# Split-array score products and split-array attention in a two-layer encoder trunk

## The chip, the cores and the metric

The kernel runs on one core of one Trainium2 chip. The metric is the device time of one execution in microseconds (us). A core has five engines with queues of their own: TensorE (matrix products; the profile lists its multiplications as PE and its loads of weights as PEld), VectorE (DVE), ScalarE (ACT), GpSimd (POOL) and SyncE (SP, which only issues DMAs here). Matrix products read SBUF and write PSUM, of which there are eight banks; the kernel hands them out one at a time (`ps`).

## The reference

A trunk of two layers is applied to two sequences of 512 and 256 tokens, 1024 wide, in float32. Each layer is half a gated feed-forward block, a token mixer, and half a feed-forward block again, each with a norm ahead of it and added to the residual:

```python
x = x + 0.5 * swiglu_ffn(rmsnorm(x, norm_g[li, 0]), ffn_w1[li, 0], ffn_w2[li, 0])
x = x + mixer(rmsnorm(x, norm_g[li, 1]))
x = x + 0.5 * swiglu_ffn(rmsnorm(x, norm_g[li, 2]), ffn_w1[li, 1], ffn_w2[li, 1])
```

The mixer of the first layer is a gated linear recurrence, run forwards and backwards with 8 heads of 128 by 128:

```python
# S_t = diag(f_t) S_{t-1} + k_t v_t^T,  o_t = S_t^T q_t,  f_t = lb + (1 - lb) sigmoid(.),  k_t = 1 - f_t
o = scan(q, k_f, i, logf_f) + reversed(scan(reversed(q), reversed(k_b), reversed(i), reversed(logf_b)))
o = (o * rsqrt(mean(o * o) + eps) * g_norm) * silu(g)
return o @ w_o
```

The mixer of the second layer is attention over a window of 128 tokens on both sides, with 16 query heads of 64, 4 key and value heads, rotation of the first 16 of each head's 64 dimensions, and one sink logit per head that joins the maximum and the denominator:

```python
s = einsum(q, k_band) * 64 ** -0.5, masked to |kpos - qpos| <= 128
m = max(max(s), sink)
p = exp(s - m);  denom = sum(p) + exp(sink - m)
o = (p / denom) @ v_band
return o @ w_o
```

## The kernel before

**Precision.** Most products are made of float32r operands: a float32 number is written as a high part `hi` (ScalarE copies and rounds, `split`, L263) and a remainder `lo` (VectorE subtracts, L264), and `mm3` (L256 to L260) adds hi x hi, hi x lo and lo x hi in PSUM. A float32r product is one record of TensorE in the profile; a product of float32 operands is two.

**Order of the work.** `tile_trunk_kernel` writes the stages one after the other: feed-forward, recurrence (`hgrn`), two feed-forward blocks, attention (`swa`), feed-forward. Inside a stage the order is written out by hand; the framework places the instructions on each engine's queue by that order and by what is ready, and adds the waits. The weights stream in through four raw buffers and are split ahead of their use.

**The recurrence.** `hgrn` (L803) makes the values, then for each head the query, and the two gates (`hgrn_proj`), then the scan (`hgrn_scan`, L676). The scan is woven with the projections of the next head (`weave`, L611): after each level of the scan, TensorE gets some pieces of those projections. The 768 tokens stand as six blocks of 128. The scan builds the matrix A of scores of each block by levels: at level l, of 0 to 6, groups of J = 2^l tokens attend to the neighbouring group, one direction for the left half and the other for the right. At each level

- ScalarE copies the keys of this level into `kop` (L699), a buffer that each level writes again;
- `scan_scores` (L670) makes one 128 x 128 product of float32 for each of the six blocks (L674): weights are the block of `kop`, data are the queries, read in place by a pattern of runs of J elements that alternates between the two directions' planes (`rhs`, L701); results go to two PSUM banks, four blocks in one and two in the other;
- `put` (L684) moves them to A, at level 0 by a copy (L688), else by a copy under a mask (L693), one instruction per bank;
- VectorE multiplies the queries (L716) and the keys (L720) in place by the gates' products, and makes the next level's products (L722).

Level 0 has a second set of scores, the diagonal, from `qs` and `kd`. After the levels come states (L744 to L755) and outputs (L768).

**Attention.** `swa` (L915) projects the keys and values; `put_kv` (L922) rotates each block of keys, splits it, writes high and low part twice each, and turns it by eight float32r transposes (`transpose_r`, L912, record line L913) into `kT`, which has the high part on both halves of the partitions and the low part likewise. Values are kept as high | low, 128 wide (`vv`). Then 24 units (4 groups of heads x 6 blocks of queries) go through `pipeline` (L1048), which sorts events by a step and a rank written out by hand, together with pieces of the query projections and, later, of the output projection. A unit (`Unit`, L1075) does

- `query`: split the four heads' queries into high | low (L263, L264); `turn`: four float32r transposes, and a copy out by ScalarE (L1100);
- `scores`, per head: two products over 128 rows (high and low query against the high part, and against the low part, of the keys; L1109, L1110), 256 or 384 keys wide; VectorE adds the band and takes the minimum (L1112);
- `exps` (L1125), `sink`, `denominator` (L1141);
- `probs`, per block of 128 keys: four float32 transposes (L1147), and a split of the result (L263, L264);
- `values`, per block: two products of 512 columns (L1159, L1160), high | low values against the high and the low probabilities;
- `finish`: ScalarE copies the lower half of the partitions (L1165) and VectorE adds it to the upper one (L1170).

`split_out` (L977) splits a group's outputs for the output projection (L986, L987), which `out_proj` (L1006) makes.

Of the kernel before, what the change touches and what calls it, by code (L numbers as in the profile page):

```python
# [47 lines left out]
class Trunk:  # L48
# [621 lines left out]
    def scan_scores(self, pss, lhs, rhs):  # L670
        nc = self.nc
        for b in range(NBLK):
            s, i = (0, b) if b < 4 else (1, b - 4)
            nc.tensor.matmul(pss[s][:, i * P : (i + 1) * P], lhs(b), rhs(b), start=True, stop=True)  # L674

    def hgrn_scan(self, hd, v):  # L676
# [7 lines left out]
        def put(level, pss):  # L684
            for s, (off, n) in enumerate(SEQS):
                dst = A[:, off : off + n]
                if level == 0:
                    nc.vector.tensor_copy(dst, pss[s])  # L688
                    continue
                nb = n // P  # L690
                m = self.masks[:, level, :].unsqueeze(1).to_broadcast([P, nb, P])
                r = lambda t: t.rearrange("p (b j) -> p b j", b=nb)
                nc.vector.copy_predicated(r(dst), m, r(pss[s]))  # L693

        tot, base = f, 0
        for l in range(LEVELS):
            c, J = T >> l, 1 << l
            kv = bass.AP(k.tensor, k.offset, [list(k.ap[0]), [2 * J, c // 2], [T + J, 2], [1, J]])
            nc.scalar.copy(kop.rearrange("p (b g j) -> p b g j", g=2, j=J), kv)  # L699

            def rhs(b):  # L701
                return bass.AP(
                    q.tensor, q.offset + b * P, [list(q.ap[0]), [2 * J, P // (2 * J)], [T + J, 2], [1, J]]
                )

            pss = [self.ps(n) for _, n in SEQS]
            self.scan_scores(pss, lambda b: blk(kop, b), rhs)
            put(l, pss)
            if l == 0:
                pss = [self.ps(n) for _, n in SEQS]  # L710
                self.scan_scores(pss, lambda b: blk(kd, b), lambda b: blk(qs, b))
                put(LEVELS, pss)
# [90 lines left out]
    def hgrn(self, lb_row, gn_row, next_row):  # L803
# [92 lines left out]
        self.drain(self.out_proj("hg_o", 0, uT, None))  # L896
        self.drain(self.out_proj("hg_o", 1, uT, next_row))

    def rotate(self, ps, heads, pos, t):
        nc = self.nc  # L900
        v = lambda t: t.rearrange("p (h d) -> p h d", d=HD)
        x, tv = v(ps), v(t)
# [12 lines left out]
    def swa(self, next_row):  # L915
# [3 lines left out]
        kT = [self.big([P, 2, T], F32R) for _ in range(KV)]  # L919
        vv = [self.big([P, 3, KV, P], F32R) for _ in range(2)]  # L920

        def put_kv(s, b, ps):  # L922
            off, n = SEQS[s]
            gb = off // P + b
            st = self.big([P, KV, 2, P], F32R)
            kh, kl = st[:, :, 0, :], st[:, :, 1, :]
            k = self.tmp(256)
            self.rotate(ps[:, :256], KV, b, k)
            self.split(k.rearrange("p (h d) -> p h d", d=HD), kh[:, :, :HD], kl[:, :, :HD])
            nc.scalar.copy(kh[:, :, HD:], kh[:, :, :HD].bitcast(F32))  # L930
            nc.scalar.copy(kl[:, :, HD:], kl[:, :, :HD].bitcast(F32))
            src = ps[:, 256:].rearrange("p (g d) -> p g d", d=HD)
            v = vv[gb // 3][:, gb % 3]
            nc.scalar.copy(v[:, :, :HD], src)
            nc.vector.tensor_sub(v[:, :, HD:], src, v[:, :, :HD].bitcast(F32))

            def rest():
                for g in range(KV):
                    pt = self.ps(256)
                    for i in range(2):  # L940
                        self.transpose_r(pt[:, i * P : (i + 1) * P], st[:, g, i, :])
                    nc.scalar.copy(kT[g][:, :, gb * P : (gb + 1) * P], pt.rearrange("p (a b) -> p a b", a=2))

            return rest
# [4 lines left out]
        def put_q(half):  # L949
            def f(s, b, ps):  # L950
# [4 lines left out]
                self.rotate(ps, 512 // HD, b, t)  # L955
# [6 lines left out]
        tiles = [None] * NC  # L962
        of = {}

        def units(gs):
            def alloc(g):
                if g not in of:
                    of[g] = self.big([P, 2, T])
                return of[g]
# [7 lines left out]
        def split_out(gs):  # L977
            for g in gs:
                for i in range(2):
                    for s, (off, n) in enumerate(SEQS):  # L980
                        if s == 0:
                            tiles[2 * g + i] = self.big([P, 2, T], F32R)
                        t = tiles[2 * g + i]
                        hi, lo = t[:, 0, off : off + n], t[:, 1, off : off + n]
                        src = of[g][:, i, off : off + n]
                        nc.scalar.copy(hi, src)  # L986
                        nc.vector.tensor_sub(lo, src, hi.bitcast(F32))  # L987

        q = itertools.chain(self.proj_tok("q0", put_q(0)), self.proj_tok("q1", put_q(1)))
        wo = self.out_proj("sw_o", 0, tiles, None)  # L990
# [6 lines left out]
        extra.append((60, lambda: split_out((0,))))  # L997
        extra.append((65, lambda: split_out((1,))))
        extra += [(66 + i * 5 / 4, piece(wo)) for i in range(24)]
        extra.append((84, lambda: split_out((2,))))  # L1000
        self.pipeline(list(units(range(KV))), extra)
        split_out((3,))
        self.drain(wo)
        self.drain(self.out_proj("sw_o", 1, tiles, next_row))

    def out_proj(self, tag, half, act, next_row):  # L1006
        for c in range(2):
            for b in range(NBLK):
                ps = self.ps()
                sl = slice(b * P, (b + 1) * P)  # L1010
                for i in range(4):
                    key = (tag, half, c, i // 2)
                    wh, wl = self.take(key)
                    t = act[half * 4 + i]
# [33 lines left out]
    def pipeline(self, units, extra):  # L1048
# [5 lines left out]
        for i, u in enumerate(units):  # L1054
# [3 lines left out]
            for h in range(GQ):  # L1058
                at(t + h // 2, 0, lambda u=u, h=h: u.scores(h))
# [15 lines left out]
class Unit:  # L1075
# [76 lines left out]
    def values(self, j):  # L1152
        k, nc = self.k, self.k.nc
        if j == 0:
            self.po = k.ps()
# [129 lines left out]
```

## Time and profile before

| | us |
|---|---|
| median of 3 runs (2833.03 to 3576.69) | 2833.57 |
| the profiled execution | 2833.56 |
| its span, first to last instruction | 2831.8 |
| recurrence, scan of the eight heads | 582 to 960 |
| attention, the units' pipeline | 2115 to 2304 |

The profile is of one execution. Its busy line gives the time that each engine worked and its share of the span; its chain follows the last instruction back through what released it. A group of instructions is named by line, engine, operation, what it writes <- what it reads, and shapes; behind the first bar stand the time that the group took in all and the mean of one in ns, behind the second bar the idle time of its engine ahead of it, and what ended that. In the view by stretches each engine has its busy time and its instruction count. In the timeline and the chain's pieces the first number is the start and the second the time taken; matrix products overlap in the pipeline, so the distance from start to start is the rate, and the time taken is longer.

### The profile page before, as it was taken

The page shows a single profiled execution, that of the slowest core. Times are in us where ns is not written, and L with a number is a line of the kernel's source. Part 1 is how long each engine was busy: PE and PEld are TensorE (multiplying, and loading weights), DVE is VectorE, ACT ScalarE, POOL GpSimd, SP SyncE. Part 2 cuts the span into 40 slices and gives each one's busy share as a digit, 9 for nine tenths or more (in the row PEclk, how much of TensorE's full clock was granted, in tenths as well). Part 3 has the DMA queues.
Part 4 walks back from the last instruction along what each step waited for, and adds up shares of the span by engine and source line. Part 5 has one row for each costly group of instructions (what it writes and reads, how often), then busy time and mean ns, then how long its engine had stood idle before and what let it go on. Part 6 is the DMA issues. An engine that isn't in the chain of part 4 may idle for free.

```text
span 2831.8 us, 40534 instructions
## 1 busy us (share of the span) xinstructions
PE 2790.5 (99%) x15225; PEld 2559.2 (90%) x15225; DVE 2203.1 (78%) x3846; ACT 1320.2 (47%) x2453; POOL 307.3 (11%) x306
## 2 busy tenths in 40 slices
PE   8999999999999999999999999999999899999998
PEld 8999999889899889999999999999887779999998
DVE  7888788477577558888878887887859978878877
ACT  7444443434344336444444643444457756434443
POOL 1111111000000001111111111111100001111110
PEclk9999999999999999999999999999999999999999
DMA  5554554311111133555454355554412113555543
GB/s 157 133 126 119 124 140 122 112 45 38 43 40 38 60 97 75 140 131 122 120 121 119 82 142 129 123 122 112 144 60 75 40 43 82 142 132 121 122 113 108
DMA packets 330100, 291.37 MB, mean 103 GB/s; under 512 B 11608, under 2 KB 257840, under 8 KB 329904
## 3 DMA queue, kind: packets, MB, share of 16 engines
q1 hardware_dynamic: 294064, 212.43, 25.6%
q0 software_dynamic: 31680, 62.93, 13.3%
q10 hardware_dynamic: 4160, 13.42, 1.3%
q8 instruction: 119, 1.95, 0.3%
q14 instruction: 77, 0.63, 0.1%
HBM read 216.39 MB, written 9.44 MB: 80 GB/s over the span
## 4 chain that ended last, share of the span: by engine, by line
PE 91%; DVE 6%; ACT 2%; issue 1%; DMA 0%; DVEq 0%; ACTq 0%; SPq 0%
PE ps L418 38%; PE ps L482 20%; PE ps L259 8%; PE ps L258 8%; PE ps L260 8%; PE ps L674 3%; PE ps L768 1%; DVE w L200 1%; DVE big L264 1%; PE ps L320 1%; PE ps L1147 1%; PE ps L744 1%; DVE w L167 0%; PE ps L1109 0%; DVE big L1112 0%
## 5 line engine op out<-in xcount | busy, mean ns | idle before, releaser
L418 PE MATMUL ps<-big,w 128*128 128x384 f32 x6720 | 1173.8, 335 | 1.5 <-ACT tA L435 1.4
L418 PEld LDWEIGHTS ps<-big,w 128*128 128x128 f32 x6720 | 1165.2, 188 | 8.4 <-ACT tA L435 6.4
L199 ACT CAST w<-wr 128x512 fp32r<-128x512 f32 x600 | 416.1, 707 | 689.2 <-DVE wr L213 342.8
L200 DVE TENSOR_TENSOR w<-wr,w 128x512 fp32r<-128x512 f32 (+1 forms) x520 | 447.8, 865 | 185.8 <-ACT w L199 174.8
L482 PE MATMUL ps<-w,big 128*128 128x512 f32 x2520 | 576.6, 390 | 0.7 <-DVE x L504 0.6
L482 PEld LDWEIGHTS ps<-w,big 128*128 128x128 f32 x2520 | 472.1, 188 | 100.1 <-ACT big L263 1.5
L504 DVE SCALAR_TENSOR_TENSOR x<-ps,x 128x512 f32<-128x512 f32 x468 | 304.3, 683 | 10.8 <-PE ps L260 10.0
L141 POOL DMA_DIRECT2D s<-wr x120 | 105.3, 877 | 1821.2 <-DMA wr<-in_ffn_w_dram 649.6
L258 PE MATMUL ps<-w,big 128*128 128x512 f32 x624 | 248.9, 399 | 0.3
L260 PE MATMUL ps<-w,big 128*128 128x512 f32 x624 | 244.9, 393 | 1.8 <-DVE big L327 1.0
L259 PE MATMUL ps<-w,big 128*128 128x512 f32 x624 | 244.2, 391 | 0.0
L258 PE MATMUL ps<-big,w 128*128 128x384 f32 (+2 forms) x640 | 221.4, 347 | 2.1 <-ACT big L263 2.0
L263 ACT CAST big<-tA 128x384 fp32r<-128x384 f32 x296 | 148.0, 513 | 151.5 <-DVE tA L450 70.3
L259 PE MATMUL ps<-big,w 128*128 128x384 f32 (+2 forms) x640 | 217.5, 340 | 0.7 <-DVE big L264 0.5
L260 PE MATMUL ps<-big,w 128*128 128x384 f32 (+2 forms) x640 | 216.3, 338 | 0.0
L264 DVE TENSOR_TENSOR big<-tA,big 128x384 fp32r<-128x384 f32 x296 | 180.3, 620 | 12.9 <-ACT big L263 12.0
L167 DVE TENSOR_TENSOR w<-wr,w 128x1024 fp32r<-128x1024 f32 x92 | 111.6, 1220 | 79.3 <-ACT w L166 73.6
L166 ACT CAST w<-wr 128x1024 fp32r<-128x1024 f32 x92 | 96.6, 1052 | 118.8 <-PE ps L259 100.2
L260 PEld LDWEIGHTS ps<-w,big 128*128 128x128 f32 x624 | 117.1, 188 | 28.0 <-DVE big L987 1.7
L200 POOL TENSOR_TENSOR w<-wr,w 128x512 fp32r<-128x512 f32 x80 | 123.8, 1547 | 166.9 <-ACT w L199 146.9
L259 PEld LDWEIGHTS ps<-w,big 128*128 128x128 f32 x624 | 117.4, 188 | 22.3
L258 PEld LDWEIGHTS ps<-w,big 128*128 128x128 f32 x624 | 117.3, 188 | 22.2 <-issue 0.3
(169 smaller groups left out, 3213.3 us busy)
## 6 DMA issues: line engine op xcount, KB each, us to landing
wr<-in_ffn_w_dram SPq DMA_DIRECT2D x264, 512.0 KB, 3.9
s<-in_ffn_w_dram SPq DMA_DIRECT2D x120, 256.0 KB, 3.3
s<-wr POOLq DMA_DIRECT2D x120, 256.0 KB, 4.4
wr<-wr POOLq DMA_DIRECT2D x80, 256.0 KB, 3.7
wr<-in_hg_w_in_dram SPq DMA_DIRECT2D x40, 512.0 KB, 3.8
wr<-wr POOLq DMA_DIRECT2D x20, 512.0 KB, 4.6
spill<-x ACTq DMA_DIRECT2D x12, 512.0 KB, 2.8
x<-spill ACTq DMA_DIRECT2D x12, 512.0 KB, 3.3
```

What stands on the lines that cost most here:

```text
L141: self.nc.gpsimd.dma_start(out, src, accum_op=ALU.add)
L167: self.nc.vector.tensor_sub(lo, raw, hi.bitcast(F32))
L199: nc.scalar.copy(h, src)
L200: low = (eng or nc.vector).tensor_sub(l, src, h.bitcast(F32)).ins
L258: nc.tensor.matmul(out, a[0], b[0], start=first, stop=False)
L259: nc.tensor.matmul(out, a[0], b[1], start=False, stop=False)
L260: nc.tensor.matmul(out, a[1], b[0], start=False, stop=last)
L263: self.nc.scalar.copy(hi, src)
L264: self.nc.vector.tensor_sub(lo, src, hi.bitcast(F32))
L418: self.nc.tensor.matmul(ps, a[x], b[y], start=first and k == 0 and i == 0, stop=k == 3 and i == 2, skip_group_check=True,)
L482: nc.tensor.matmul(ps, a[x], w[y], start=name == chain and kp == 0 and q == 0, stop=kp == 1 and q == 2, skip_group_check=True,)
L504: self.nc.vector.scalar_tensor_tensor(x, ps, c, x, ALU.mult, ALU.add)
```

## The change

Products that fill only half of TensorE's array, by columns or by rows, are issued in pairs that lie in different halves.

- **Scan, scores.** Each block's 128 x 128 product becomes two products of 64 columns of weights by 64 queries (`par` 0 and 1); their results lie in partitions 0 to 63 and 64 to 127 of one PSUM bank for all six blocks. `put` has one instruction per half of the partitions; at level 6 it is a plain copy.
- **Scan, queries.** At levels 1 to 5 ScalarE copies the queries into `qop`, in contiguous rows, as it does the keys; `qop` is in turn `kd` and `qs`, which are free after level 0. Levels 0 and 6 read the queries in place.
- **Keys and values.** `put_kv` no longer splits; GpSimd writes the rotated keys a second time, four float32 transposes turn them, and the split follows from PSUM. The values are kept whole, 64 wide, in float32.
- **Units.** `query` is gone; `turn` makes two float32 transposes and then a split. `scores` takes two heads at a time: the three products hi x hi, hi x lo and lo x hi over 64 rows each, one head on the upper and one on the lower half of the rows, into two PSUM banks. `probs` only copies. `values` makes two float32 products of 64 columns of weights by 256 of data, into the two halves of the partitions. `finish` splits straight into the output projection's operands; `split_out` is gone.
- `out_proj` takes its operands from a function; the products that it makes are the same.

```diff
-    def scan_scores(self, pss, lhs, rhs):
-        nc = self.nc
+    def scan_scores(self, lhs, rhs):
+        ps = self.ps(NBLK * 64)
         for b in range(NBLK):
-            s, i = (0, b) if b < 4 else (1, b - 4)
-            nc.tensor.matmul(pss[s][:, i * P : (i + 1) * P], lhs(b), rhs(b), start=True, stop=True)
+            for par in range(2):
+                rows = slice(par * 64, (par + 1) * 64)
+                self.nc.tensor.matmul(ps[rows, b * 64 : (b + 1) * 64], lhs(b)[:, rows], rhs(b, par), start=True, stop=True)
+        return ps
...
+            packed = 0 < l < LEVELS - 1
+            if packed:
+                qop = (qs, kd)[l % 2]
+                qv = bass.AP(q.tensor, q.offset, [list(q.ap[0]), [2 * J, c // 2], [T + J, 2], [1, J]])
+                nc.scalar.copy(qop.rearrange("p (b g j) -> p b g j", g=2, j=J), qv)
...
-            st = self.big([P, KV, 2, P], F32R)
...
+            st = self.tmp(512).rearrange("p (g a d) -> p g a d", a=2, d=HD)
+            self.rotate(ps[:, :256], KV, b, st[:, :, 0, :])
+            nc.gpsimd.tensor_copy(st[:, :, 1, :], st[:, :, 0, :])
+            nc.scalar.copy(vv[:, gb], ps[:, 256:].rearrange("p (g d) -> p g d", d=HD))
...
+    def turn(self):
         k = self.k
-        q = self.q().rearrange("p (h d) -> p h d", d=HD)
-        self.st = k.big([P, GQ, P], F32R)
-        k.split(q, self.st[:, :, :HD], self.st[:, :, HD:])
...
+        pt = k.ps(256)
+        q = self.q()
+        for i in range(2):
+            k.nc.tensor.transpose(pt[:, i * P : (i + 1) * P], q[:, i * P : (i + 1) * P], k.ident)
+        t = k.tmp(512, F32R)
+        self.qT = t[:, :256], t[:, 256:]
+        k.split(pt, *self.qT)
...
-        nc.tensor.matmul(ps, qi, self.kT[:, 0, self.keys], start=True, stop=False)
-        nc.tensor.matmul(ps, qi, self.kT[:, 1, self.keys], start=False, stop=True)
...
+        for j, (x, y) in enumerate(((0, 0), (0, 1), (1, 0))):
+            for par in range(2):
+                rows = slice(par * HD, (par + 1) * HD)
+                q = self.qT[x][rows, p * P : (p + 1) * P]
+                nc.tensor.matmul(pss[par], q, self.kT[y][rows, self.keys], start=j == 0, stop=j == 2)
...
-        hi, lo = k.tmp(512, F32R), k.tmp(512, F32R)
-        k.split(pt, hi, lo)
-        self.split[j] = (hi, lo)
...
+        self.pT[j] = k.tmp(512)
+        k.nc.scalar.copy(self.pT[j], pt)
...
-        nc.tensor.matmul(self.po, v, hi, start=(j == 0), stop=False)
-        nc.tensor.matmul(self.po, v, lo, start=False, stop=(j == self.nkb - 1))
+        for par in range(2):
+            nc.tensor.matmul(
+                self.po[par * HD : (par + 1) * HD, :],
+                v,
+                self.pT[j][:, par * 256 : (par + 1) * 256],
+                start=j == 0,
+                stop=j == self.nkb - 1,
+                skip_group_check=True,
+            )
...
     def finish(self):
-        k, nc = self.k, self.k.nc
-        low = k.tmp(512)
-        nc.scalar.copy(low[:HD, :], self.po[HD:, :])
...
+        self.k.split(self.po.rearrange("p (c q) -> p c q", c=2), *(t[:, :, lo : lo + P] for t in self.of()))
```

In `pipeline` the turn of a unit's queries stands three steps ahead of its scores, where the split stood, and each of the two pairs of heads has the step that its two heads had.

More of the change, by code (lines that the diff above doesn't have):

```diff
@@ L960, in put_q @@
             return f
-        tiles = [None] * NC
         of = {}
@@ L967, in alloc @@
                 if g not in of:
-                    of[g] = self.big([P, 2, T])
+                    of[g] = [self.big([P, 2, T], F32R) for _ in range(2)]
                 return of[g]
```

163 lines of the change are left out of this document (65 added, 98 removed).

## The prediction

> **What bounds the kernel now.** I read the page's busy line and chain first, then the busy time of the two stages that the change touches, and last the groups and the timeline of their matmuls.
>
> ```profile
> span 2831.8 us, 40534 instructions
> PE 2790.5 (99%) x15225; PEld 2559.2 (90%) x15225; DVE 2203.1 (78%) x3846; ACT 1320.2 (47%) x2453; POOL 307.3 (11%) x306
> PE 91%; DVE 6%; ACT 2%; issue 1%; DMA 0%; DVEq 0%; ACTq 0%; SPq 0%
> ```
>
> TensorE ends 91% of the chain, so a change is worth what it takes off TensorE's queue, wherever TensorE is the engine that is never late. The busy time by stretch says where that is: the recurrence's scan (582 to 960 us) and the pipeline of attention units (2115 to 2304 us).
>
> ```profile
> core 0: us, PE busy (x) PEld busy (x) DVE busy (x) ACT busy (x) POOL busy (x), PEclk, DMA share, GB/s
> 667.66:710.30 42.64, 42.64 (x294) 39.34 (x293) 33.55 (x59) 17.45 (x34) 0.00 (x0) 1.00 0.13 38
> 2115.00:2304.00 189.00, 172.96 (x952) 141.70 (x951) 172.77 (x538) 136.52 (x362) 0.00 (x0) 0.99 0.16 51
> 582.00:960.00 378.00, 377.94 (x2466) 343.74 (x2465) 276.92 (x487) 150.47 (x264) 0.00 (x0) 1.00 0.14 39
> ```
>
> The first row is one head of the scan: TensorE has no gap in 42.6 us, VectorE is busy 33.6 and ScalarE 17.5. In attention TensorE stands idle for 189.0 - 173.0 = 16.0 us, and VectorE (172.8) is as full as TensorE. What TensorE waits for there is VectorE's work in line: the split of the queries, and the scaling of the probabilities.
>
> ```profile
> PE ps L913 <- DVE big L264: 8.5, 6, 3.6
> PE ps L1147 <- DVE big L1141: 2.1, 2, 1.8
> ```
>
> **The rates that price the edits.** These are the chain's pieces of the scan (a float32 product is two MATMUL records, so one level's six blocks are 12), and the timeline of TensorE in attention.
>
> ```profile
> 667.66 3.33 PE ps L674 x24
> 675.26 1.44 PE ps L674 x12
> 679.44 1.34 PE ps L674 x12
> 2106.02 0.28 PE L1110 MATMUL ps<-big,tA 128*128 128x256 f32 x1
> 2106.14 0.28 PE L1109 MATMUL ps<-big,tA 128*128 128x256 f32 x1
> 2111.30 0.34 PE L1110 MATMUL ps<-big,tA 128*128 128x384 f32 x1
> 2111.47 0.34 PE L1109 MATMUL ps<-big,tA 128*128 128x384 f32 x1
> 2103.39 0.39 PE L260 MATMUL ps<-w,big 128*128 128x512 f32 x1
> 2103.62 0.40 PE L258 MATMUL ps<-w,big 128*128 128x512 f32 x1
> ```
>
> A float32 record of 128 columns takes 1.34/12 = 0.112 us. The first piece is level 0 and the diagonal blocks together: less 1.34 leaves 1.99 us for level 0, 0.166 us a record, because its queries are read in runs of one element; level 1, in runs of two, costs 0.120. The float32r records (one per product) start 0.12, 0.17 and 0.23 us apart at 256, 384 and 512 columns. A record of 512 columns lasts 0.39 us though the next starts after 0.23, so some 0.16 us of each is pipeline that the next one covers.
>
> **Scan, matrix work.** Scores per head now: 1.99 + 1.34 (diagonal) + 1.44 + 5 x 1.34 = 11.5 us. After, each block is two products of 64 columns by 64 queries, whose results lie in different partitions: 24 records a level instead of 12, each half as long: 0.112/2 plus 2 ns for the fixed part, 0.058 us; 0.086 at level 0. No row of this trace has fewer than 128 columns of weights, so whether the two halves run side by side has to be bounded. One end: one after the other, 24 x 0.058 = 1.39 us a level, no gain. The other: side by side, 12 x 0.058 = 0.70. Records start in order and the queue holds first half, first half, second half, second half, so a group has a lone record at each end: 13 slots, 0.75 us. I take that, as the halves share neither columns of the array nor partitions of PSUM, and the nearest row for the loads lets them through:
>
> ```profile
> 2102.55 0.46 PE L913 MATMUL ps<-ident_r,big 128*128 128x128 f32 x4
> 2102.85 0.47 PE L258 MATMUL ps<-w,big 128*128 128x512 f32 x1
> ```
>
> four transposes, each with a load of 128 columns, in 0.30 us: at most 0.075 us a load, so 24 loads of 64 columns need some 0.9 us if strictly one by one, and less as they overlap. After: 7 x 13 x 0.058 + 13 x 0.086 = 6.4 us a head, a saving of 5.1.
>
> Against it stands the **change of shape**: before and after each group the array goes from whole to split. The lower bound is next to nothing (a float32 group between float32r ones now loses about 0.02 us); the upper is the 0.16 us of pipeline above, if the array has to empty. I take 0.06, nearer to the low end, because weights and data of the next shape can enter before the last sums have left. Level 0 and the diagonal go together, so a head has 7 groups, 14 changes, 0.84 us.
>
> The Trainium skill, TensorEngine Tiling (Array Packing), section "Tiling Modes", states that going from one tiling mode to another drains TensorE, and that different tiles load and multiply in parallel. No run here shows either so far; by the first the price is the upper bound of 0.16 us, and that is a rival below.
>
> **Scan, the other engines.** The change adds one ScalarE copy of the queries at levels 1 to 5: 40 copies. Evacuation keeps its two instructions per set of scores, of 64 partitions by 384 instead of 128 by 512 and by 256.
>
> ```profile
> L699 ACT COPY big<-big 128x768 f32<-128x768 f32 x56 | 50.3, 898 | 91.0 <-PE ps L674 66.4 <-issue 13.6 <-DVE big L720 5.7
> L693 DVE COPY_PREDICATED big<-big,ps 128x512 f32<-128x512 uint8 x56 | 41.4, 740 | 41.8 <-PE ps L674 41.2 <-issue 0.5
> L693 DVE COPY_PREDICATED big<-big,ps 128x256 f32<-128x256 uint8 x56 | 24.5, 438 | 0.0
> ```
>
> 40 x 0.898 = 36 us of ScalarE, 4.5 a head: 22 busy of some 38, hidden under the next head's projections on TensorE. Were that cover gone, its place is in line behind the copy of the keys, which now already waits for the scores (66.4 us in total): 5 x 0.9 = 4.5 us a head. Evacuation: halfway between 0.438 and 0.740 is 0.589, times two 1.178, which is 0.740 + 0.438: nothing. The copy lets VectorE multiply the queries in place before the scores are read. VectorE stays at 33.6 in some 38.4, 87%, so I allow 0.5 us a head for TensorE waiting on it. Scan: (5.1 - 0.84 - 0.5) x 8 = **-30 us**.
>
> **Attention, matrix work.** These are the groups by line that fall or change; 24 units, of which 16 see 256 keys and 8 see 384; 56 blocks of probabilities.
>
> ```profile
> L1109 PE MATMUL ps<-big,tA 128*128 128x256 f32 x64 | 17.1, 293 | 0.3 <-ACT tA L1100 0.2
> L1109 PE MATMUL ps<-big,tA 128*128 128x384 f32 x32 | 10.9, 340 | 0.1
> L1159 PE MATMUL ps<-tA,big 128*128 128x512 f32 x56 | 24.3, 435 | 0.6 <-ACT tA L263 0.6
> L913 PE MATMUL ps<-ident_r,big 128*128 128x128 f32 x144 | 16.7, 246 | 10.3 <-DVE big L264 8.5 <-ACT tA L263 1.6
> L1147 PE MATMUL ps<-ident_r,big 128*128 128x128 f32 x224 | 33.8, 279 | 2.3 <-DVE big L1141 2.1
> 2113.93 1.04 PE L1147 MATMUL ps<-ident_r,big 128*128 128x128 f32 x8
> 2114.72 0.47 PE L258 MATMUL ps<-w,big 128*128 128x512 f32 x1
> ```
>
> Scores now: L1109 and L1110, 128 x 0.12 + 64 x 0.174 = 26.5 us. After: three products on each half of the rows, two heads side by side, three slots where four were: -6.6 (one by one: +13.2). The queue alternates the halves here, so there is no lone record. Values now: L1159 and L1160, 2 x 0.227 = 0.454 us a block. After: float32 against 64 columns of weights, 256 columns of data, two records per half at 0.218 (as 512 of float32r, less a little); order first, first, second, second: three slots, 0.654, so **+0.2 x 56 = +11.2** (two slots: -1; four: +23). Transposes of the queries: four float32r at about 0.084 become two float32 at 0.109 (eight L1147 in the 0.79 us of its rows, with the 0.08 by which the next record is late): -2.8. Changes of shape: 48 groups of scores and 56 of values, 208 x 0.06 = +12.5. Keys, before this stretch: 48 transposes become 24: -1.4.
>
> So TensorE in the stretch: 173.0 - 6.6 + 11.2 - 2.8 + 12.5 = 187.3 us.
>
> **Attention, the other engines.** VectorE loses these:
>
> ```profile
> L264 DVE TENSOR_TENSOR tA<-ps,tA 128x512 fp32r<-128x512 f32 x56 | 38.3, 687 | 3.0 <-ACT tA L263 2.5
> L264 DVE TENSOR_TENSOR big<-x,big 128x256 fp32r<-128x256 f32 x12 | 5.0, 415 | 0.5 <-ACT big L263 0.5
> L1170 DVE TENSOR_TENSOR big<-ps,tA 64x256 f32<-64x256 f32 x48 | 19.9, 415 | 4.3 <-ACT tA L1165 3.7
> L987 DVE TENSOR_TENSOR big<-big,big 128x512 fp32r<-128x512 f32 x8 | 5.5, 686 | 0.0
> ```
>
> 38.3 + 2 x 5.0 (the second half of the queries has a like group) + 19.9 + 5.5 x 1.6 (with L987's shorter form) = 77, and gains two subtractions of 256 a unit, 48 x 0.42 = 20: 57 less, 116 us. ScalarE (136.5 of 189.0) gains two casts of 256 a unit and loses those of the queries, of the split outputs and the half-height copies: not more than now. With VectorE at 60% the waits above go; I leave a quarter of the 16 us idle, 4. Stretch: 187.3 + 4 = 191.3 for 189.0: **+2.3**. VectorE's relief is real, but TensorE takes its place as the bound.
>
> **Sum.** -30 + 2.3 - 1.4 = -29. The profiled execution took 2833.56 us around its span of 2831.8, and the median of the runs is 2833.57, so the sum is made against that: **2805 us**. A measurement of this kernel tells about 2%, 57 us, from no change.
>
> **The rivals.**
> (a) Halves overlap without edges and shape changes cost nothing. For it: no row now shows a change of operand kind costing over 0.02 us. Against it: order first, first, second, second. Scan 7 x 12 x 0.058 + 12 x 0.086 = 5.9 of 11.5, -44.6; attention 173.0 - 6.6 - 1 - 2.8 + 4 = 166.6, -22.4; -1.4: 2765 us.
> (b) The array empties at every change: 320 changes (112 + 208) x 0.10 more = +32: 2837 us. For it: 0.16 us of each matmul is covered by its follower only. Against: nothing in the trace.
> (c) The slower end: the halves run one after the other. Per head 7 x 24 x 0.058 + 24 x 0.086 + 0.84 = 12.65 for 11.5, +9.4 in all; attention 173.0 + 13.2 + 23.4 - 2.8 + 12.5 + 4 = 223.3, +34.3; -1.4: 2876 us. It decides once some two fifths of the pairs don't overlap (29 of the 71 us between the ends). For it: both halves of a level stream over the same 128 rows. Against: the loads, above.
> (d) The scan's chain takes TensorE's place. The timeline of VectorE in one level:
>
> ```profile
> 676.26 1.06 DVE L693 COPY_PREDICATED big<-big,ps 128x512 f32<-128x512 uint8 x2 [0.17 <-PE ps L674]
> 677.22 0.94 DVE L716 TENSOR_TENSOR big<-big,big 128x768 f32<-128x768 f32 x1
> ```
>
> Scores, evacuation (1.06), product of the queries (0.94), packing (0.9) and the next scores follow each other: 2.9 us, 3.1 with waits between engines, against 4.18 - 1.44 = 2.7 us of projections between two groups of the chain: 0.4 x 6 x 8 = +19: 2824 us. For it: this is VectorE's order now. Against: the product no longer needs the scores to be read, so it can go ahead of the evacuation.
>
> **Chances.** Forecast 0.50 with its own range 2785 (shape changes free) to 2828; (a) 0.20, (b) 0.12, (c) 0.12, (d) 0.06. The range runs from just below (a) to short of (c): 2758 to 2852. Faster by over 2%: most of (a) and a little of the forecast, 0.22; slower: half of (c) and a little of (b), 0.07; within 2%: 0.71.
>
> **What would show it.** Right: score groups of about 0.75 us a level with pairs of records a few ns apart, a head in 38 to 39 us, VectorE in attention under 65%, value groups near 0.65 us, and gaps below 0.1 us where shapes change. Wrong: level groups of 1.3 us or more (c), gaps of 0.15 us around every group (b), TensorE waiting for ScalarE's packing (d), or an attention stretch under 170 us (a).

## The result and the profile after

The changed kernel takes 2799.76 us (median of 4 runs, 2798.89 to 2800.6), the kernel before 2833.57 us beside it: a ratio of 0.9876, 95% interval [0.9857, 0.9895]. Two runs far from all others, 3576.69 us of the kernel before in this series and 9801.9 us of `halves_apart` below, are left out of the medians. The forecast was 2805 us, 29 us off; measured, 33.8 us are off, by the medians and by the spans of the two profiled executions (2831.8 and 2798.0). The page of the changed kernel, its busy line and its chain:

```profile
span 2798.0 us, 42188 instructions
PE 2769.8 (99%) x16129; PEld 2492.3 (89%) x16129; DVE 2163.1 (77%) x3750; ACT 1315.9 (47%) x2423; POOL 308.1 (11%) x312
PE 92%; DVE 5%; ACT 2%; DMA 1%; issue 1%; DVEq 0%; ACTq 0%; SPq 0%
```

The whole execution says little: TensorE is still busy 99% of it, with 904 more records and 20.7 us less work. From the last matrix product of the feed-forward block ahead of the recurrence to the first one behind it, the time falls from 608.3 to 583.7 us (-24.6); the same stretch around attention falls from 342.1 to 334.0 (-8.1). 1.1 us of the 33.8 lie elsewhere. The busy time by stretch, of the changed kernel for one head of the scan and for the units' pipeline, from the first score product to the last value product:

```profile
core 0: us, PE busy (x) PEld busy (x) DVE busy (x) ACT busy (x) POOL busy (x), PEclk, DMA share, GB/s
659.55:699.12 39.57, 39.56 (x391) 34.29 (x392) 34.88 (x59) 21.49 (x39) 0.00 (x0) 1.00 0.15 41
2078.40:2264.90 186.50, 184.81 (x1142) 124.11 (x1143) 131.72 (x470) 116.29 (x341) 0.00 (x0) 1.00 0.15 48
```

And of the kernel before, the same pipeline cut in the same way (columns as above):

```profile
2105.40:2299.95 194.55, 178.51 (x988) 146.77 (x988) 177.52 (x563) 142.48 (x378) 0.00 (x0) 0.99 0.16 50
```

A head of the scan took 42.64 us and takes 39.5, and TensorE has no gap in it before or after: there the change is worth only what it takes off TensorE. In attention it is the other way round: TensorE's work rises by 6.3 us (178.5 to 184.8), but its idle time falls from 16.0 us to 1.7, because VectorE has 46 us less to do. The whole gain of attention, 8.05 us, lies in this pipeline. What TensorE still waits for there, with the waits' total, count and longest, in the view of waits:

```profile
PE ps L1081 <- DVE big L919: 1.0, 1, 1.0
PE ps L1081 <- DVE x L919: 0.4, 1, 0.4
PE ps L1146 <- ACT tA L1138: 0.3, 1, 0.3
```

The waits that the prediction named, on the split queries (8.5 us) and on the scaled probabilities (2.1), are gone.

**The granted clock** takes a small share. The first row is of the kernel before at the start of the scan, the second of the same kernel inside the units' pipeline, in the view by stretches (the clock is the third number from the end of a row):

```profile
582.00:612.00 30.00, 30.00 (x201) 28.03 (x200) 23.68 (x42) 9.82 (x13) 0.00 (x0) 0.95 0.12 36
...
2225.00:2255.00 30.00, 27.30 (x146) 22.30 (x146) 27.84 (x89) 19.74 (x56) 0.00 (x0) 0.97 0.11 36
```

30 us at 0.95 are 1.5 us lost; in the pipeline 30 us at 0.98 (2195 to 2225) and 30 at 0.97 are 1.5 more. The changed kernel has 1.00 in both stretches. So of the 24.6 some 23.1, and of the 8.1 some 6.6, belong to the work. The medians hold such a share too: the kernel before ran at a mean clock of 0.994 to 0.998 in the runs beside the experiments, 2838 us at the lowest and 2830 to 2833 at 0.998; the changed kernel ran at 0.998 to 0.999. At 0.998 in both, the difference is 30 to 33 us.

**One group of scores.** The chain's pieces at level 0 with the diagonal, and at two later levels:

```profile
659.63 1.85 PE ps L675 x48
665.93 0.85 PE ps L675 x24
669.73 0.85 PE ps L675 x24
```

They stand against 3.33 and 1.34 us for twice as wide records before. The timeline around one of these groups, with the load of its first weights:

```profile
665.54 0.39 PE L260 MATMUL ps<-big,w 128*128 128x512 f32 x1
665.86 0.78 PEld L675 LDWEIGHTS ps<-big,big 128*64 128x64 f32 x24 [0.36 <-issue]
665.86 0.92 PE L675 MATMUL ps<-big,big 128*64 128x64 f32 x24
666.71 0.50 PE L258 MATMUL ps<-big,w 128*128 128x512 f32 x1
667.05 0.39 PE L259 MATMUL ps<-big,w 128*128 128x512 f32 x1
```

Two things can be read here. The starts of the first records, read one by one, come in pairs: 665.863 and 665.870, 665.970 and 665.977, 666.028 and 666.035, 666.087 and on. Two halves run side by side, 6 to 7 ns apart, and the next pair follows after 0.0584 us; the first pair has no lone record ahead of it, so 24 records are 12 slots. And the group costs more than its slots. A record of 512 columns is followed by its like after 0.23 us; here the group begins 0.32 after it (+0.09), holds the chain 0.85 for 12 x 0.058 = 0.70 of slots (+0.15), and the record behind it is followed after 0.34 (+0.11). That makes 0.35 us for going into the split array and out again, **0.17 us for each change of shape**. The load's row shows a part of it: the first weights of the group are loaded only when its first product starts, 0.32 us after the product ahead began, and the unit that loads stood idle 0.36 us ahead of that. Float32 behind float32r is not the reason: the first weights of such a group in the kernel before, whole, were loaded at 679.06, 0.22 us ahead of its first product.

### The profile page after: what moved, and what is told of

It reads as the page before. It is cut to its first block, busy times and chain, and to the rows that moved or that the text cites. A ratio compares the mean times of both kernels' runs of the same rounds, so it can differ in the third digit from the quotient of the medians.

```text
span 2798.0 us, 42188 instructions
## 1 busy us (share of the span) xinstructions
PE 2769.8 (99%) x16129; PEld 2492.3 (89%) x16129; DVE 2163.1 (77%) x3750; ACT 1315.9 (47%) x2423; POOL 308.1 (11%) x312
## 4 chain that ended last, share of the span: by engine, by line
PE 92%; DVE 5%; ACT 2%; DMA 1%; issue 1%; DVEq 0%; ACTq 0%; SPq 0%
PE ps L418 39%; PE ps L482 20%; PE ps L258 9%; PE ps L260 8%; PE ps L259 8%; PE ps L675 2%; PE ps L1146 1%; PE ps L1096 1%; PE ps L777 1%; PE ps L1136 1%; DVE w L200 1%; PE ps L320 1%; DMA wr<-wr 1%; PE ps L753 1%; DVE big L264 1%
## 5 line engine op out<-in xcount | busy, mean ns | idle before, releaser
L482 PEld LDWEIGHTS ps<-w,big 128*128 128x128 f32 x2520 | 472.2, 188 | 101.2 <-ACT big L263 2.7
L504 DVE SCALAR_TENSOR_TENSOR x<-ps,x 128x512 f32<-128x512 f32 x468 | 303.5, 681 | 10.4 <-PE ps L260 10.0
L258 PEld LDWEIGHTS ps<-w,big 128*128 128x128 f32 x624 | 117.2, 188 | 30.0 <-issue 6.5
L260 PEld LDWEIGHTS ps<-w,big 128*128 128x128 f32 x624 | 117.1, 188 | 27.1 <-DVE big L327 1.7
L141 POOL DMA_DIRECT2D wr<-wr x100 | 87.4, 874 | 447.9 <-ACT w L199 165.9
```

Of the source, the lines that this page charges most:

```text
L141: self.nc.gpsimd.dma_start(out, src, accum_op=ALU.add)
L258: nc.tensor.matmul(out, a[0], b[0], start=first, stop=False)
L260: nc.tensor.matmul(out, a[1], b[0], start=False, stop=last)
L482: nc.tensor.matmul(ps, a[x], w[y], start=name == chain and kp == 0 and q == 0, stop=kp == 1 and q == 2, skip_group_check=True,)
L504: self.nc.vector.scalar_tensor_tensor(x, ps, c, x, ALU.mult, ALU.add)
```

## The experiments

Theory A: in the scan the gain is 12 paired slots a group less 0.17 us for every change of shape; in attention it is the work taken from VectorE, and the split products there cost TensorE time. Theory B: the changes of shape are nearly free, and either contiguous queries (packing) or better overlap makes the scan's gain. Differences to the changed kernel are taken between medians of different series, in which the kernel before stood between 2832.68 and 2834.96, so 2 us of such a difference mean nothing. The two stretches in the traces are finer: outside them the twelve traced executions took 1877.3 to 1881.6 us, though no edit changes the work there.

**The two parts alone.** `scan_only` is the kernel before with the changed kernel's `scan_scores` and `hgrn_scan`; `attn_only` is the changed kernel with these two as before. The cores of the two edits, against the changed kernel:

```diff
scan_only
-    def turn(self):
+    def query(self):
+    def turn(self):
...
+            st = self.big([P, KV, 2, P], F32R)
attn_only
-    def scan_scores(self, lhs, rhs):
+    def scan_scores(self, pss, lhs, rhs):
...
+            nc.tensor.matmul(pss[s][:, i * P : (i + 1) * P], lhs(b), rhs(b), start=True, stop=True)
```

> The kernel before with the changed scan alone (split score products, packed queries); attention as before. Theory 1, from the two traces (a pair of half products costs one slot of 0.058 us, each change of the array's shape about 0.17 us): the scan is 25 us shorter, so 2811 us. Rival, that the changed scan and the changed attention share a gain that neither has alone (the weights' staging ahead): less than 15 us, over 2820.

> The changed kernel with the scan as before; attention changed. Theory 1: TensorE has more to do in the units' pipeline (6 us) and stops waiting for VectorE (14 us), so about 8 to 10 us shorter than before, 2826. Rival, that TensorE's rates in attention gain by the split products themselves: 15 us or more.

`scan_only` took 2808.23 us, ratio 0.9913 [0.9898, 0.9927] (-24.5); `attn_only` 2822.33 us, 0.9961 [0.9946, 0.9976] (-10.4), both beside 2832.68. The stretch of the recurrence is 583.7 us in the first, that of attention 334.0 in the second, each as in the changed kernel. (The traced execution of `scan_only` is its longest, 2812.05; its attention, which is that of before, took 347.0 us, and the clock from 2070 to 2320 us was 0.97.) The sum of the two, -34.9, is the whole gain within those 2 us: the parts don't help or hinder each other.

**Are the halves side by side because of their order?** All first halves of a level are issued ahead of all second halves:

```diff
-        for b in range(NBLK):
-            for par in range(2):
+        for par in range(2):
+            for b in range(NBLK):
```

> The changed kernel with the six blocks of the first half queued ahead of the six of the second, so that neighbours in the queue lie in the same half of the array. Theory 1 (the gain is two neighbours running side by side): a score group grows from 12 slots of 0.058 us to 24, by 0.7 us, level 0 by 0.9; 8 heads x (7 x 0.7 + 0.9) = 46 us more, 2846, slower than before. Rival (a half-wide product is simply cheaper, neighbour or not): no change, 2800.

It took 2831.7 us, 0.9996 [0.9986, 1.0006]: the whole gain of the scan and what attention gives besides are gone. The chain's pieces of this kernel, level 0 first:

```profile
666.80 2.79 PE ps L675 x45
674.04 1.36 PE ps L675 x24
678.36 1.36 PE ps L675 x24
```

1.36 us a level for 0.85, and 2.79 for 1.85: 8 heads x (6 x 0.51 + 0.94) = 32 us, which is what was measured (2831.7 - 2799.8). So the overlap is shown, and it depends on neighbours in the queue lying in different halves. It is 32 us and not the expected 46 because the runs of one half are not wholly apart. The timeline gives the group from 673.98 to the next record at 675.34:

```profile
673.66 0.39 PE L260 MATMUL ps<-big,w 128*128 128x512 f32 x1
673.98 1.43 PE L675 MATMUL ps<-big,big 128*64 128x64 f32 x24
675.34 0.50 PE L258 MATMUL ps<-big,w 128*128 128x512 f32 x1
```

The trace does not name the half of a record, but the spacing tells them apart. Twelve of the 24 starts follow each other at 0.058 us behind a first step of 0.107: 673.975, 674.082 and so on to 674.548, 674.607 and 674.665. The other twelve do the same from 674.496 (674.602, 674.661 and on). So the second half begins ahead of the last three records of the first: three pairs form at the seam, and 21 slots are left of 24. That reading also explains the missing lone records of the changed kernel: a float32 product is two records, queued first, first, second, second, and the second half's start beside the first half's all the same. The Trainium skill, "TensorE: Matmul & The Clock Gate", section "Part 3: Packing small matmuls — row/col tiling", says that products start strictly in their order. By that rule a group would have a lone record at each end, 13 slots; these starts show that records in another half of the columns can go ahead of some queued earlier, and the measurement decides.

**Is it the contiguous queries?** The packing is left out, and all levels read the queries in place:

```diff
-            packed = 0 < l < LEVELS - 1
+            packed = False
```

> The changed kernel without the packing copies: at levels 1 to 5 TensorE reads the queries in place by runs of 2 to 32. Theory 1: only level 1 has a slower slot (0.062 for 0.058), and VectorE's product of the queries waits for the scores again; the chain scores, evacuation, product, scores of 2.2 us fits in the 2.7 us of projections, so within 5 us of the changed kernel, 2795 to 2808. Rival (the forecast's chain takes TensorE's place, or two streams over the same rows slow short runs): 0.4 us a level, 15 to 20 us more.

It took 2799.67 us, 0.9881 [0.9866, 0.9896], no different from the changed kernel. Pieces of its chain, level 0, 1 and 2:

```profile
659.38 1.85 PE ps L675 x48
665.68 0.90 PE ps L675 x24
669.52 0.85 PE ps L675 x24
```

Only level 1, which reads in runs of two elements, is dearer, by 0.05 us, 0.4 us over the eight heads; from level 2 on, reading in place costs nothing that these pieces show. The stretch of the recurrence is 584.9 us for 583.7. Theory B's packing is not the cause.

**What does a change of shape cost?** To each group of levels 1 to 6 one whole-array product of float32 is added whose result nobody reads: in `dummy_end` behind the last block, where the array has to change anyway, in `dummy_mid` between blocks 2 and 3, where that makes two changes more. The work is the same in both.

```diff
+        if extra:
+            spare = self.ps(P)
...
dummy_end
+            if extra and b == NBLK - 1:
+                self.nc.tensor.matmul(spare, lhs(0), lhs(1), start=True, stop=True)
dummy_mid
+            if extra and b == 2:
+                self.nc.tensor.matmul(spare, lhs(0), lhs(1), start=True, stop=True)
```

> The changed kernel with one whole float32 product of 128 by 128 by 128 more, its result unread, behind each score group of levels 1 to 6 (48 of them). Both theories: two records of 0.112 us each, 48 x 0.22 = 11 us more than the changed kernel, 2811.

> The same extra product in the middle of each of these groups, behind the third block, so that the array changes shape twice more per group. Theory 1 (a change of shape costs 0.17 us): 48 x 0.34 = 16 us more than with the product at the end, 2827. Rival (the time lost around a group belongs to its first product's waits and its operands, not to the shape): within 3 us of the product at the end.

`dummy_end` took 2806.64 us, 0.9903 [0.9886, 0.9919]; `dummy_mid` 2825.57 us, 0.9972 [0.996, 0.9983]. 48 groups with two changes more differ by 18.9 us, 0.20 us a change by the medians. The traces are finer. One head, from its first score product to that of the next, in `dummy_end` and in `dummy_mid`, columns as above:

```profile
661.93:702.74 40.81, 40.81 (x401) 35.54 (x400) 35.14 (x59) 21.15 (x38) 0.00 (x0) 1.00 0.13 40
665.41:708.30 42.89, 42.89 (x402) 36.48 (x401) 35.25 (x59) 21.18 (x38) 0.00 (x0) 1.00 0.13 38
```

Twelve changes more are 2.08 us: **0.17 us a change**, with the work held equal. The whole stretch of the recurrence, 593.5 and 609.9 us, gives the same (16.4/96); the rest of the medians' 18.9 lies where the two kernels are alike. One group of `dummy_end` in its chain:

```profile
668.30 0.85 PE ps L677 x24
669.15 0.42 PE ps L679 x2
```

and one of `dummy_mid`:

```profile
671.78 0.50 PE ps L677 x12
672.28 0.42 PE ps L679 x2
672.70 0.50 PE ps L677 x12
```

Half a group is six slots, 0.35 us, and holds the chain 0.50. The added product, 0.42 us in both places, is two records that take 0.22 between their likes. In `dummy_end` a head is 1.3 us longer than the 39.5 of the changed kernel, for six products: 0.22 us each, their two records and nothing besides. Theory A stands, Theory B's free changes fall.

**Fewer changes, same work.** If a change costs that much, attention should gain by standing its split groups together. `merged` starts both pairs of a unit's scores in one step and puts a unit's value groups into one step:

```diff
-                at(t + h, 0, lambda u=u, h=h: u.scores(h))
+                at(t, 0, lambda u=u, h=h: u.scores(h))
...
-                at(t + 7 + j, 4, lambda u=u, j=j: u.values(j))
+                at(t + 6 + u.nkb, 4, lambda u=u, j=j: u.values(j))
```

> The changed kernel with fewer groups in attention: the two pairs of a unit's scores stand together, and the two or three value products of a unit stand together behind its last block of probabilities: 24 + 24 groups instead of 48 + 56. Theory 1: 56 groups fewer x 0.34 us = 19 us less, 2781, if VectorE keeps up (70% busy now). Rival (TensorE's waits come back, as four score banks and three blocks of probabilities come due at once): no gain, 2795 to 2805.

It took 2788.92 us, 0.9839 [0.9825, 0.9854], 10.8 us less than the changed kernel. Counted along TensorE's records, attention goes from 163 changes to 93; 10.8/70 is 0.155 us each (0.14 by the 9.7 us of TensorE's busy time below). The stretch of attention falls by 9.3 us, from 334.0 to 324.8, 0.13 a change; but 30 us of it (2170 to 2200) ran at a clock of 0.94, and with those 1.8 us it would be 0.16. The size was expected larger because I had counted two changes for every group that moves, and many of them already stood beside another split group. The pipeline's stretch in `merged`, columns as above:

```profile
2078.40:2256.20 177.80, 175.07 (x1145) 128.90 (x1145) 130.89 (x470) 116.39 (x342) 0.00 (x0) 0.99 0.16 52
```

TensorE works 175.1 us instead of 184.8 on the same products. The groups by line show where. In the changed kernel, over this stretch:

```profile
L258 PE MATMUL ps<-w,big 128*128 128x512 f32 x121 | 53.4, 441 | 0.0
L1146 PE MATMUL ps<-tA,big 128*64 128x256 f32 x222 | 36.1, 404 | 0.3 <-ACT tA L1138 0.3
L1096 PE MATMUL ps<-big,tA 64*128 64x256 f32 x192 | 19.6, 310 | 0.0
```

and in `merged`:

```profile
L258 PE MATMUL ps<-w,big 128*128 128x512 f32 x121 | 53.6, 443 | 0.0
L1146 PE MATMUL ps<-tA,big 128*64 128x256 f32 x224 | 29.7, 390 | 0.2 <-ACT tA L1138 0.2
L1096 PE MATMUL ps<-big,tA 64*128 64x256 f32 x192 | 15.6, 294 | 0.0
```

The split groups lose 6.4 and 4.0 us of busy time (the first row lacks two records, which its window cuts off); the whole-array projections beside them stay as they were.

**Is the rest of attention VectorE's relief?** The changed kernel's `probs` only copies. `dve_back` gives VectorE a subtraction of 512 columns per block again, as the split had; nobody reads its result:

```diff
+        k.nc.vector.tensor_sub(k.tmp(512), pt, self.pT[j])
```

> The changed kernel with one more subtraction of 128 by 512 on VectorE behind each block of probabilities, its result unread: 56 x 0.69 = 38 us of VectorE in attention again, as before the change. Theory 1 (attention gains because TensorE no longer waits for VectorE, while the split products cost TensorE more than they save): most of the 8 us are gone, 2804 to 2812. Rival (the split products are the gain): under 2 us more than the changed kernel, 2800.

It took 2807.11 us, 0.9903 [0.9888, 0.9918], 7.35 us more than the changed kernel, and the stretch of attention is 341.3 us, against 334.0 and, before the change, 342.1. The pipeline:

```profile
2078.40:2273.00 194.60, 190.22 (x1143) 126.73 (x1139) 163.57 (x526) 117.04 (x340) 0.00 (x0) 0.98 0.16 48
```

With 32 us back on VectorE (163.6) the pipeline is as long as before, 194.6 us, though TensorE's own products are those of the changed kernel. But the clock of 0.98 in this row has to be taken off first. Of the same kernel:

```profile
2200.00:2230.00 30.00, 28.83 (x156) 19.92 (x157) 21.88 (x73) 13.32 (x43) 0.00 (x0) 0.89 0.06 19
```

30 us at 0.89 are 3.3 us. By the whole stretch of attention, 341.3 less 3.3 is 4.0 us more than the changed kernel's 334.0, where the kernel before, less its 1.5, was 6.6 more. By the pipeline, cut here too at its first score product, 0.7 us earlier than the row, 195.3 less 3.3 is 5.5 us more than 186.5, where the kernel before was 6.5 more. So 32 of the 46 us of VectorE's work, 70%, bring back 60 to 85% of what attention gained. The subtraction puts back more than VectorE's time: it also holds the PSUM bank that it reads, as the split did. But where TensorE's idle time grows, from 1.7 to 4.4 us, it waits mostly for VectorE's rotation of the queries (L919) and not for a bank:

```profile
PE ps L1081 <- DVE big L919: 2.4, 1, 2.4
PE ps L1081 <- DVE x L919: 0.9, 1, 0.9
```

VectorE's relief is the cause, shown by putting most of it back; that all of it would bring back all is not tried.

**The two last steps.** `adjacent` puts a unit's value group right behind the scores of the unit after next, which leaves 76 changes; `adjacent_strided` is that without the packing.

```diff
adjacent
-                at(t + 7 + j, 4, lambda u=u, j=j: u.values(j))
-            at(t + 6 + u.nkb, 4, u.finish)
+                at(t + 8, 0.5, lambda u=u, j=j: u.values(j))
+            at(t + 8, 0.5, u.finish)
adjacent_strided, besides
-            packed = 0 < l < LEVELS - 1
+            packed = False
```

> As the run with fewer groups, but with a unit's value products right behind the scores of the unit after next, so that the array goes whole, split by rows, split by columns, whole: three changes a unit instead of four. Theory 1: 24 to 26 changes fewer than there, at 0.15 to 0.19 us: 4 us less, 2785. Rival (going from one split to the other costs as much as through the whole array): 2789.

> The same without the packing copies of the scan. Theory 1 (packing neither costs nor gains): as the run with neighbouring groups, 2785. Rival (packing hides a wait that shows once other time is gone): 5 us or more above it.

`adjacent` took 2788.16 us (2786.68 to 2790.12), 0.9838 [0.9822, 0.9855]: `merged` and it can't be told apart by their medians, though its stretch of attention is 1.1 us shorter (323.6 for 324.8), where 17 changes less at 0.155 would be 2.6; TensorE's waits in the pipeline are 1.1 us longer there (3.8 for 2.7). `adjacent_strided` took 2791.35 us (2789.57 to 2791.93), 0.9847 [0.9832, 0.9862], 3.2 us more: between what the two readings gave, and the intervals overlap. The stretches of the recurrence differ by 0.9 us (584.8 for 583.9), as 1.2 in `strided`: the packing is worth about 1 us there, and the rest of the 3.2 lies outside the two stretches. `merged` and `adjacent` are both faster than the changed kernel, by some 11 us.

## Why the prediction came out as it did

The time lay 5 us under the forecast, inside its own range. That it came so near is in part luck: the scan gave 5.4 us less than its term and attention 10.4 us more. That the scan gives most of the gain was right, as was its mechanism. The terms that failed were the price of a change of shape (too low), the slots of a group (too many), and attention's sum, which had the wrong sign.

**Scan, -30 forecast, -24.6 measured,** or -23.1 without the clock's share. The step "a group has a lone record at each end: 13 slots" failed: there are 12, and 7 x 0.70 + 12 x 0.0845 = 5.9 us a head, where 6.4 were put, save 5.55 of 11.5. "I take 0.06" for a change of shape failed more: 0.17, so 14 changes are 2.4 us a head and not 0.84. The allowance of "0.5 us a head for TensorE waiting on" VectorE was not needed in most heads: in the one shown VectorE is busy 34.9 us of 39.6, 88%, as forecast, and TensorE has no gap. 5.55 - 2.4 = 3.15 us a head, and 42.64 - 39.5 is measured; eight times that is 25, some 2 more than the stretch shows. Most of it is lost in the seventh head, which takes 41.13 us for 42.9 before and gains only 1.8. There TensorE does wait, 1.4 us, for the copies of the queries (L707) and of the keys (L702). Its row in the view by stretches, columns as above, and its waits:

```profile
850.36:891.49 41.13, 39.69 (x389) 34.16 (x389) 35.65 (x60) 22.80 (x43) 0.00 (x0) 1.00 0.14 40
...
PE ps L675 <- ACT big L707: 0.7, 1, 0.7
PE ps L675 <- ACT big L702: 0.7, 2, 0.5
```

The reason that I gave for 0.06, that weights and data of the next shape can enter before the last sums have left, is what failed: the load's row above begins only with its own product.

The other engines came out as worked out. In the groups by line, the evacuation and the packing:

```profile
L696 DVE COPY_PREDICATED big<-big,ps 64x384 f32<-64x384 uint8 x96 | 57.0, 594 | 15.1 <-PE ps L675 13.0
L707 ACT COPY big<-big 128x768 f32<-128x768 f32 x40 | 34.2, 855 | 43.6 <-DVE big L725 43.5
```

0.594 us was put at 0.589, and the 40 copies at 36 us are 34.2; but for the 0.7 us of the seventh head and 0.3 in the eighth they lie under the projections, and `strided`, without them, is not faster (in its seventh head TensorE waits 2.1 us for other work of ScalarE).

**Attention, +2.3 forecast, -8.05 measured,** or -6.6 without the clock's share. "VectorE's relief is real, but TensorE takes its place as the bound" was half right: TensorE is now busy 184.8 of 186.5 us, and that bound is lower than I put it. Idle time: 4 us forecast, 1.7 measured. TensorE's work: +14.3 forecast, +6.3 measured. The "three slots, 0.654" for a block of values failed in the same way as the lone records. A stretch of the changed kernel's timeline where values and scores stand side by side:

```profile
2152.12 0.39 PE L260 MATMUL ps<-w,big 128*128 128x512 f32 x1
2152.44 0.65 PE L1146 MATMUL ps<-tA,big 128*64 128x256 f32 x4
2153.02 0.61 PE L1096 MATMUL ps<-big,tA 64*128 64x256 f32 x6
2153.57 0.33 PE L1136 MATMUL ps<-ident_r,big 128*128 128x128 f32 x1
```

The four value records are two pairs (2152.437 and .443, 2152.703 and .710), two slots and not three, and the group ends after 0.58 us with its way in included. The six score records take 0.55 us. The three slots of about 0.11 forecast for the scores are there too (the third pair starts 0.117 after the second, the second 0.22 after the first with the way in, 3 to 4 ns lie within a pair). But four whole records of scores were 0.48 us before; three slots and two changes, 0.35 + 0.34, are 0.69, so a pair of heads whose group has both changes to itself loses by the split.

Of the 8 us by which TensorE's forecast was off, the values' third slot is -12.2 (+11.2 put, -1 found) and the changes are +12.8 (163 at 0.155 for 208 at 0.06), so these two cancel. What is left, some 8 us, I can only argue: the records of before, at the rates that the prediction quotes, fill 169 of TensorE's 178.5 busy us, and I carried the other 10 over as if they stayed. 1.5 of them are the clock; records drawn out ahead of a wait count as busy too, and those waits have gone. No run tests this. The keys' -1.4 isn't seen: outside its pipeline the attention stretch is 147.5 us before and after.

**The rivals.** (a) had no edges right and free changes wrong. (b) had the price of a change right, 0.16 us, against the row that I preferred; its 2837 us came out wrong because it kept the 13th slot, the third slot of the values and 320 changes, where there are 275 (112 in the scan, 163 in attention). These make 23 of its 37 us too many; the rest is the 0.5 us a head, the idle time and the 8 us above. The Trainium skill, "TensorEngine Tiling (Array Packing)", section "Tiling Modes", which stood beside it, says that a change of mode drains TensorE and that tiles work in parallel; the trace is in keeping with the first, at 0.13 to 0.17 us a change, and shows the second, with 3 to 7 ns between the starts of two halves. (c), one half after the other, is `halves_apart` and not this kernel. (d) is not there in the head shown, where TensorE is busy 39.56 of 39.57 us, but it shows in the seventh: the chain of copies costs TensorE 1.4 us there.

Of the signs that the prediction named, pairs a few ns apart were seen, and TensorE waits for the packing only in the last two heads, 1.1 us in all. A group is 0.85 us and not 0.75, a head 39.5 us and not 38 to 39, a value group 0.58 and not near 0.65, VectorE in attention 71% (131.7 of 186.5) and not under 65%. That last one is a slip of counting: 57 us were taken off as a sum of instruction times, and such a sum does fall by 55 (213 to 158), but the busy time, in which instructions that overlap count once, falls by 46. And the gaps at the changes are the 0.09 to 0.15 us that were to speak for (b).

## What to carry to other kernels

Splitting TensorE's array for half-sized products halves their time only inside a group; every group pays some 0.34 us for going in and out. Here a scan group of 1.34 us gains 0.3 net and a score group of 0.48 us alone loses 0.2, so put split groups side by side (70 changes fewer in attention gave 11 us) and alternate the halves in the queue. Where another engine is as full as the matrix engine, its relief can be worth more than the matrix work that the same edit saves or adds: put that work back alone, as `dve_back` does, to know which it was.

## What the runs showed of the hardware

- A change between the whole and the split array costs 0.17 us at a scan group, the same with work held equal, and 0.13 to 0.16 us where 70 were taken away. It is no row of its own: it lies in later starts of the records on both sides and in idle time of the weight loads.
- Two halves split by columns start 6 to 7 ns apart, two split by rows 3 to 4 ns, and records of one half can start ahead of earlier ones of the other: 21 slots for 24 records in `halves_apart`.
- Queries read in runs of one element cost 0.166 us a whole record before, for 0.112 in contiguous runs. In the split array two such streams side by side take 0.0845 us, and one alone 0.084 in `halves_apart`: two slow streams don't slow each other.
- The granted clock falls in short stretches whose place differs between the traced executions, one of each kernel: 0.95 at the start of the scan in the kernel before and in `attn_only`, which has its scan, but 1.00 there in the changed kernel and in `scan_only`; 0.89 over 30 us of the pipeline in `dve_back`, where the changed kernel has 1.00. In a narrow window each is some 3.4 us at 0.50 (581.70 to 585.10 in the kernel before), or 6.8 in `dve_back`. Each costs 1 to 4 us, as much as the smaller terms here, so a stretch is compared with its clock beside it. What sets them was not looked into.
